# Two-layer hybrid block on one core: the modulation product spread over four column strips from its own ring of buffers, and the last layer's output projection in a written order

## Chip, cores, metric

One core of one Trainium2 chip. The metric is the device time of one execution in microseconds (us).

## The reference

Two layers over 256 latent and 256 context tokens of width 1024. What matters here:

```python
for i in range(DEPTH):
    mod = (s_lat @ ada_w[i] + ada_b[i])          # 1024 -> 6144, one row each for
    mod_c = s_ctx @ ada_w[i] + ada_b[i]          # latent and context
    sh1, sc1, g1, sh2, sc2, g2 = jnp.split(mod, 6, -1)
    u = modulate(h, sh1, sc1)
    # u @ w_in, four token mixers, gates: mix = merged @ w_out
    h = layer_norm(DN_ALPHA * h + g1 * mix, ln1_g[i], ln1_b[i])
    f = conv_ffn(modulate(h, sh2, sc2), ffn_w_up[i], ...)   # up 1024 -> 2*2816, conv, SwiGLU, down
    h = layer_norm(DN_ALPHA * h + g2 * f, ln2_g[i], ln2_b[i])
```

`modulate` is `layer_norm(x) * (1 + scale) + shift`. The last layer computes only the latent tokens from the mixers on (token tiles 2 and 3, 128 tokens each).

## The kernel before

All products with weights are "dense": a weight tile of 128x1024 (512 KB) is loaded by SyncE into the tag `w` (three buffers, `wload`, L190), cut into a rounded high part by ScalarE (`whi`, L197) and a low part by VectorE or GpSimd (`wlo`, L201; two buffers each), and multiplied in three passes per 128 rows of depth: high weight by high activation, high by low, low by high (`mm`, L174). One column tile is 24 matmuls of 512 tokens in layer 0 and of 256 tokens in layer 1.

The modulation (`ada`) is 12 groups per layer. A group is four weight tiles (`adaw`) of 128x1024. Its stationary operand is `sst`, 128x32: only two of its 32 columns are not zero (latent and context). A matmul of it fills one of four strips of 32 columns of the array, and so 32 of 128 partitions of a bank of PSUM. In the kernel before a tile holds two depths k by 512 columns, so that tile c uses strips 0 and 1 or strips 2 and 3:

```python
for k in (2 * c, 2 * c + 1):
    g = k % 4
    self.mm(ps[32 * g:32 * g + 32, :], self.sst[:, k, :], w[:, k % 2 * 512:k % 2 * 512 + 512], k < 4, k >= 4)
yield 0.4
```

After four tiles come a copy (`adas`), four transposes (L178), a sum over the strips (L388) and the bias. `ada` is a generator. `col_tile` draws `rate` steps from it (`self.side`) per column tile of dense work, so that its loads and matmuls stand between those of the dense work, and its tiles use the same three buffers `w`. In layer 0, groups 0 to 3 come first of all, groups 4 to 9 beside the columns of the Hyena and RWKV mixers, and 10 and 11 beside the context's up projection. Layer 1's groups 0 to 3 stand in layer 0's up projection; 4 to 9 beside layer 1's columns for RWKV, Hyena and the window attention; 10 and 11 behind layer 1's output projection, where `backbone` runs them with nothing beside them.

The last layer's output projection (`out_proj`) runs over eight depths for token tiles 2 and 3 and over two halves of 512 columns. `tail` then does for each tile: gate and residual (L1666, L1668), a LayerNorm from sums (`sum_stats`: a square on ScalarE L440, the power -0.5 on GpSimd L443; `post_norm`: L1620, L1625), a second LayerNorm without weights (L455), eight transposes (L178), and scale and shift into `uh` and `ul` (L475, L476, L478). The up projection starts when `uh` and `ul` are there for both tiles. Its first four weight tiles are loaded and cut ahead (`ph`, `pl`).

A scheduler sets the order of the instructions on each engine when the program is built, by its own estimates. Inside `manual_schedule` the engines that are named keep the order in which the program is written. Each engine then runs its own list in order; SyncE's list holds the DMA issues, and a DMA that waits for a buffer holds back those behind it.

Of the kernel before, what the change touches and what calls it, by code (L numbers as in the profile page):

```python
# [8 lines left out]
F32 = mybir.dt.float32  # L9
F32R = mybir.dt.float32r  # L10
# [145 lines left out]
class Net:  # L156
    def __init__(self, ctx, tc, a, out):
        self.ctx, self.tc, self.nc, self.a, self.out = ctx, tc, tc.nc, a, out
        self.work, self.pre, self.pool_cols = [], [], 0
        self.side, self.rate = iter(()), 0  # L160
        self.lo = self.nc.vector
        self.aside, self.done, self.feed = [], set(), None
# [199 lines left out]
    def ada(self, l, groups, early=False):  # L362
# [6 lines left out]
        for g4 in groups:  # L369
            ps = self.bank("d")  # L370
            for c in range(4):
                n = g4 * 4 + c
                tag = ("w", "whi", "wlo", "w", "whi", "w", "wlo")[n % 7] if early else "w"
                w = self.wp.tile([128, 1024], F32, tag=tag, name=tag, bufs=3 if tag == "w" else 2)
                nc.sync.dma_start(w, self.a["adaw"][l, n])
                for k in (2 * c, 2 * c + 1):
                    g = k % 4
                    self.mm(ps[32 * g:32 * g + 32, :], self.sst[:, k, :], w[:, k % 2 * 512:k % 2 * 512 + 512],
                            k < 4, k >= 4)
                yield 0.4  # L380
            sb = self.wp.tile([128, 512], F32, tag="adas", name="adas", bufs=1)
            nc.scalar.copy(sb, ps)
# [16 lines left out]
    def gate_out(self, l, n0, scale):  # L399
# [6 lines left out]
        r = self.wp.tile([16, 128], F32, tag="gr", name="gr", bufs=1)  # L406
# [1296 lines left out]

    def ffn_up(self, l, pool, units, room, hid, hidp, more):
# [36 lines left out]
def backbone(ctx, tc, a, out):  # L1741
# [6 lines left out]
    for l in range(DEPTH):  # L1748
# [5 lines left out]
        N.side = N.ada(l, range(4 if l else 4, 10))  # L1754
        ox = ExitStack()
        if 1:
            with ExitStack() as mx:
# [3 lines left out]
                with ExitStack() as hp:  # L1761
                    qh, qr = [], {}
                    if l:
                        rp = lower()
                        N.rwkv_tiles(l, rp, rp, qr)
                        N.rate = 1
# [4 lines left out]
                        hcx.close()  # L1771
                    hk = hp.enter_context(tc.tile_pool(name="hk", bufs=1, side="right"))
# [74 lines left out]
                    N.rate = (1 if l else 2)  # L1847
# [12 lines left out]
                    N.weave(N.rwkv_prep(l, rp, hq, need_ctx, qr), 0.5)  # L1860
                    N.flush()
# [6 lines left out]
                with ExitStack() as ax:  # L1868
# [6 lines left out]
                    N.weave(N.side, 0.0)  # L1875
                    N.gate_out(l, 16, 0.5)
                    N.rate = 0
# [49 lines left out]
        lg, lb = (op.tile([128, 1024], F32, name=x) for x in ("lg", "lb"))  # L1927
# [16 lines left out]
        def tail(its):  # L1944
            xs = []
            for i, sums in its:
# [8 lines left out]
        N.weave(N.out_proj(l, op, lambda k: a["wout"][l, k], 8, lambda k: ahl[k], tiles, N.h, g1, tail,  # L1955
                           (2 if need_ctx else 5), hooks(), l == 1 and 0), 0.4)
# [145 lines left out]
```

## Time and profile before

| | us |
|---|---|
| median of 3 runs | 1859.11 (1858.53 to 1861.16) |
| the profiled execution | 1862.13 |
| its span, first to last instruction | 1860.1 |
| TensorE matmul (PE) busy | 1702.9 (92%) |
| TensorE weight load (PEld) busy | 1354.4 (73%) |
| VectorE (DVE) busy | 1145.5 (62%) |
| ScalarE (ACT) busy | 787.3 (42%) |
| GpSimd (POOL) busy | 641.4 (34%) |
| HBM read | 235.84 MB, 128 GB/s over the span |

The profiled execution took 2.0 us more than its span, and 3.0 us more than the median. A share of busy time is an average over stages with different limits; a stage is read with the table of stretches and the list of instructions in order of time.

### The profile page before, as it was taken

The numbers are of one execution on the slowest core, as the hardware profiler recorded it, in microseconds if no ns is written. First come the engines' busy times: TensorE is split into PE (matmuls) and PEld (weight loads), VectorE is DVE, ScalarE is ACT, GpSimd is POOL, SyncE is SP. The second block draws the span as 40 slices with busy tenths as digits, with TensorE's granted clock in tenths as the row PEclk, the third lists the DMA queues.
The fourth block names the chain that finished last, engine by engine and source line by source line (L and its number), as shares of the span: only waits on it lengthen the run. The fifth ranks groups of instructions, "written<-read, shape, count | busy, mean of one in ns | idle before, by whom it ended". The sixth has DMA issues, their size and how long they took to land.

```text
span 1860.1 us, 36364 instructions
## 1 busy us (share of the span) xinstructions
PE 1702.9 (92%) x14618; PEld 1354.4 (73%) x14618; DVE 1145.5 (62%) x2204; ACT 787.3 (42%) x1579; POOL 641.4 (34%) x782
## 2 busy tenths in 40 slices
PE   6999999998999988999999998899788998879987
PEld 2566778776777766877787776677687887679964
DVE  5566456775665478544555657563765665758887
ACT  2323345653232346433334444334553343356632
POOL 2313144544544126101010164244454664131153
PEclk9999999999999999999999999999889999889999
DMA  8353321211111455344334556653123222646543
GB/s 302 126 198 113 130 69 57 83 57 45 45 56 55 148 196 189 120 150 139 125 102 138 180 175 210 198 179 130 47 88 97 88 65 82 237 142 189 184 145 113
DMA packets 73456, 241.37 MB, mean 130 GB/s; under 512 B 8518, under 2 KB 17096, under 8 KB 73032
## 3 DMA queue, kind: packets, MB, share of 16 engines
q1 hardware_dynamic: 69336, 229.80, 37.6%
q10 hardware_dynamic: 3952, 9.25, 1.5%
q8 instruction: 115, 1.88, 0.4%
q14 instruction: 53, 0.43, 0.1%
HBM read 235.84 MB, written 2.13 MB: 128 GB/s over the span
## 4 chain that ended last, share of the span: by engine, by line
PE 60%; DVE 15%; ACT 5%; DMA 4%; POOL 3%; issue 3%; POOLq 0%; SPq 0%; ACTq 0%; DVEq 0%
PE bkd L174 45%; PE bkm L174 8%; PE bkm L1362 2%; PE bko L174 2%; DVE wlo L201 2%; PE bkm L178 2%; ACT whi L197 2%; DMA w<-in_wdn 1%; DMA w<-in_wout 1%; DMA w<-in_win 1%; DVE sV L1340 1%; DVE dmx L978 1%; ACT dp L981 1%; POOL wlo L201 1%; DMA w<-in_adaw 1%
## 5 line engine op out<-in xcount | busy, mean ns | idle before, releaser
L174 PE MATMUL bkd<-uh,whi 128*128 128x256 f32 (+1 forms) x1624 | 585.7, 361 | 7.1 <-ACT whi L197 3.3
L174 PE MATMUL bkd<-uh,wlo 128*128 128x256 f32 (+1 forms) x1624 | 555.4, 342 | 3.5 <-DVE wlo L201 3.2
L174 PE MATMUL bkd<-ul,whi 128*128 128x256 f32 (+1 forms) x1624 | 552.9, 340 | 0.0
L197 ACT CAST whi<-w 128x256 fp32r<-128x256 f32 (+1 forms) x532 | 333.7, 661 | 268.4 <-PE bkd L174 116.6
L201 DVE TENSOR_TENSOR wlo<-w,whi 128x1024 fp32r<-128x1024 f32 (+3 forms) x247 | 284.2, 1155 | 195.7 <-ACT whi L197 194.8
L201 POOL TENSOR_TENSOR wlo<-w,whi 128x256 fp32r<-128x256 f32 (+2 forms) x328 | 276.9, 863 | 314.2 <-ACT whi L197 307.6
L174 PEld LDWEIGHTS bkd<-uh,whi 128*128 128x128 f32 x1624 | 311.8, 192 | 85.1 <-ACT whi L197 24.0
L174 PEld LDWEIGHTS bkd<-uh,wlo 128*128 128x128 f32 x1624 | 311.7, 192 | 40.8 <-DVE wlo L201 3.8
L174 PEld LDWEIGHTS bkd<-ul,whi 128*128 128x128 f32 x1624 | 312.9, 193 | 26.6 <-issue 0.7
L1722 POOL TENSOR_TENSOR fc<-fc,fc 128x256 f32<-128x256 f32 (+1 forms) x47 | 46.2, 982 | 331.3 <-DVE fc L329 312.0
L174 PE MATMUL bkd<-w,sst 128*32 128x512 f32 x348 | 81.0, 646 | 18.3 <-DMA w<-in_adaw 18.2
L1584 POOL TENSOR_TENSOR acc<-acc,tg 128x512 f32<-128x512 f32 (+1 forms) x32 | 32.5, 1017 | 145.4 <-DVE tg L1583 132.4
L324 ACT ACTIVATE fc<-bkd,vec 128x256 f32<-128x256 f32 (+1 forms) x94 | 60.8, 647 | 7.5 <-PE bkd L174 7.5
L327 DVE SCALAR_TENSOR_TENSOR fc<-bkd,vec,fc 128x255 f32<-128x255 f32 (+1 forms) x94 | 54.8, 583 | 11.5 <-ACT fc L324 11.5
L174 PE MATMUL bkd<-wlo,hh 128*128 128x512 f32 x126 | 52.4, 416 | 9.3 <-DVE wlo L201 6.2
L237 ACT CAST hh<-fc 128x256 fp32r<-128x256 f32 (+1 forms) x47 | 23.2, 493 | 84.9 <-POOL fc L1722 84.9
L329 DVE SCALAR_TENSOR_TENSOR fc<-bkd,vec,fc 128x255 f32<-128x255 f32 (+1 forms) x94 | 55.3, 589 | 2.9
L238 DVE TENSOR_TENSOR hl<-fc,hh 128x256 fp32r<-128x256 f32 (+1 forms) x47 | 25.6, 545 | 47.4 <-ACT hh L237 47.4
L174 PE MATMUL bkd<-y,wbh 128*128 128x512 f32 (+1 forms) x192 | 54.6, 369 | 0.0
L238 DVE TENSOR_TENSOR wbl<-wb,wbh 128x256 fp32r<-128x256 f32 x48 | 29.3, 611 | 37.0 <-ACT wbh L237 36.7
L174 PE MATMUL bkd<-whi,hh 128*128 128x512 f32 x126 | 48.5, 399 | 3.7 <-DVE fc L329 2.3
L981 ACT ACTIVATE dp<-bkm,dmx 128x512 f32<-128x512 f32 (+1 forms) x48 | 29.6, 617 | 48.2 <-DVE dmx L979 40.2
(474 smaller groups left out, 2995.6 us busy)
## 6 DMA issues: line engine op xcount, KB each, us to landing
w<-in_adaw SPq DMA_DIRECT2D x87, 512.0 KB, 3.9
w<-in_wup SPq DMA_DIRECT2D x82, 512.0 KB, 3.5
w<-in_wdn SPq DMA_DIRECT2D x66, 512.0 KB, 3.5
w<-in_wg SPq DMA_DIRECT2D x64, 512.0 KB, 3.5
w<-in_win SPq DMA_DIRECT2D x58, 512.0 KB, 3.6
w<-in_wout SPq DMA_DIRECT2D x24, 512.0 KB, 3.6
wb<-in_wbr SPq DMA_DIRECT2D x48, 128.0 KB, 3.4
pw<-in_wup SPq DMA_DIRECT2D x8, 512.0 KB, 4.5
```

Of the source, the lines that this page charges most:

```text
L174: self.nc.tensor.matmul(out, lhsT, rhs, start=start, stop=stop)
L178: self.nc.tensor.transpose(out, in_, self.ident[0:n, 0:n])
L197: self.nc.scalar.copy(hi[:, c], w[:, c])
L201: e.tensor_tensor(lo[:, c], w[:, c], hi[:, c].bitcast(F32), ALU.subtract)
L238: nc.vector.tensor_tensor(lo, src, hi.bitcast(F32), ALU.subtract)
L324: nc.scalar.activation(dst, ps, AF.Identity, bias=b, scale=w1)
L327: nc.vector.scalar_tensor_tensor(d3[:, :, 1:256], p3[:, :, 0:255], w0, d3[:, :, 1:256], ALU.mult, ALU.add)
L329: nc.vector.scalar_tensor_tensor(d3[:, :, 0:255], p3[:, :, 1:256], w2, d3[:, :, 0:255], ALU.mult, ALU.add)
L981: nc.scalar.activation(p[:, 0:n], ps[:, 0:n], AF.Exp, scale=scale, bias=mx[:, hc], accum_out=zz[:, hc])
L1362: nc.tensor.matmul(ps[r, o:o + 32], L(r, d, c, x, e, j), R[r, d, 2 * e + j, :], start=True, stop=True, tile_position=(r.start, r.start))
L1584: nc.gpsimd.tensor_tensor(acc, acc, tg[:, 0:n], ALU.add)
L1722: nc.gpsimd.tensor_tensor(ab[0], ab[0], ab[1], ALU.mult)
```

## The change

- `adaw` is packed anew: a tile holds four depths by 256 columns. Each tile gives four matmuls of 256 columns, one for each strip, in place of two of 512 columns on two strips. The bytes, the tiles and the products are the same.
- `ada` can take its tiles from a ring of four buffers of its own (`ew`), and yields after one, two or four tiles (`at_once`). `rate` may be a fraction.
- Layer 0's groups 4 to 9 and layer 1's last groups come from the ring, four tiles at once. Layer 1's groups 0 to 7, not 0 to 3, stand in layer 0's up projection, two tiles at once; groups 8 to 11 stand beside layer 1's Hyena and RWKV columns. Beside layer 1's first six column tiles, and behind its output projection, there are none any more.
- The last layer's `out_proj` and `tail` are replaced by `last_proj`, written out for PE, DVE, ACT and POOL: token tile 2 over all eight depths, then tile 3 by halves; tile 2's norms stand beside tile 3's matmuls; then the first three up tiles on tile 2's 128 tokens, tile 3's norms, and the other 128 tokens of these up tiles (`begun`, drawn by `col_tile`).

The diff, cut to its core:

```diff
     def col_tile(self, src, part):
+        if self.begun:
+            rest_, ps = self.begun.pop(0)
+            yield from rest_
+            return ps
         hi, lo = self.wsplit(src)
-        for _ in range(self.rate):
+        self.due += self.rate
+        while self.due >= 1:
+            self.due -= 1
             next(self.side, None)
...
-                tag = ("w", "whi", "wlo", "w", "whi", "w", "wlo")[n % 7] if early else "w"
-                w = self.wp.tile([128, 1024], F32, tag=tag, name=tag, bufs=3 if tag == "w" else 2)
+                half, h = divmod(c, 2)
+                if ring:
+                    w = ring.tile([128, 1024], F32, tag="ew", name="ew", bufs=4)
...
-                for k in (2 * c, 2 * c + 1):
-                    g = k % 4
-                    self.mm(ps[32 * g:32 * g + 32, :], self.sst[:, k, :], w[:, k % 2 * 512:k % 2 * 512 + 512],
-                            k < 4, k >= 4)
-                yield 0.4
+                for g in range(4):
+                    self.mm(ps[32 * g:32 * g + 32, half * 256:half * 256 + 256], self.sst[:, 4 * h + g, :],
+                            w[:, g * 256:g * 256 + 256], h == 0, h == 1)
...
+                if (c + 1) % at_once == 0:
+                    yield 0.4 * at_once
...
-        N.side = N.ada(l, range(4 if l else 4, 10))
...
+                    ring = hp.enter_context(tc.tile_pool(name="ring", bufs=1, side="right"))
+                    N.side = N.ada(l, range(8, 12) if l else range(4, 10), ring=ring, at_once=4)
...
-                    N.rate = (1 if l else 2)
+                    N.rate = 0.65 if l else 0.8
...
-            N.rate = 1 if l == 0 and kc < k else 2 if part is CTX and k < kc - 1 else 0
+            N.rate = 0.7 if l == 0 and kc < k else 2 if part is CTX and k < kc - 1 else 0
...
-            N.weave(N.ada(l, (10, 11)), 0.0)
-            N.gate_out(l, 40, 1.0)
...
-                    N.side = N.ada(1, range(4))
+                    N.side = N.ada(1, range(8), at_once=2)
...
+            N.last_proj(l, op, fw, ahl, N.h, g1[1], 3)
```

The order of `last_proj` (its helpers do the arithmetic of `out_proj` and `tail`; `cut` loads and cuts one weight tile, `up_cut` a tile of the up projection in quarters, `norms` is a generator over both LayerNorms of a tile):

```python
            self.pool_cols = 256
            cut(0)
            cut(1)
...
            for k in range(8):
                if k < 6:
                    cut(k + 2)
                step(2, k)
            self.pool_cols = 0
            left = [(hf, k) for hf in range(2) for k in range(8)]
            for hf, k in left[:14]:
                step(3, k, [hf])
            cuts = [up_cut(x, nc.vector if x == 1 else nc.gpsimd) for x in range(nup)]
            go(cuts[0])
            gated(2, 0)
            gated(2, 1)
            xn = [P("xn", 1024) for _ in range(2)]
            n2, n3 = norms(2, xn[0]), norms(3, xn[1])
            go(n2, 2)
            go(cuts[1], 1)
            go(n2, 1)
            go(cuts[1])
            go(cuts[2], 2)
            go(n2)
            go(cuts[2])
            gated(3, 0)
            m2 = self.modulate(pool, l, 1, xn[:1], 2)
            next(m2)
            for hf, k in left[14:]:
                step(3, k, [hf])
            go(m2, 6)
            gated(3, 1)
            go(n3, 2)
            go(m2)
            for hi, lo in ups:
                bk = self.bank("d")
                part = lambda c, t0, t1, bk=bk, hi=hi, lo=lo: self.dense(bk[:, c:c + 128], hi, lo, lambda k: k * 128,
                                                                         self.uh, self.ul, 8, t0, t1)
                for _ in part(0, 256, 384):
                    pass
                self.begun.append((part(128, 384, 512), bk[:, 0:256]))
            go(n3)
            for _ in self.modulate(pool, l, 1, xn[1:], 3):
                pass
```

What the change moves, at three places. First SyncE's list in layer 1's columns. The names are target, source: `w<-in_win` is a dense weight tile, `adaw` a modulation tile. Before:

```order
L375 DMA w<-in_adaw 128x1024
L190 DMA w<-in_win 128x1024
L375 DMA w<-in_adaw 128x1024
L190 DMA w<-in_win 128x1024 x2
L375 DMA w<-in_adaw 128x1024
```

and now:

```order
L190 DMA w<-in_win 128x1024 x3
L206 DMA wb<-in_wbr 128x256 x2
L190 DMA w<-in_win 128x1024 x6
L387 DMA ew<-in_adaw 128x1024 x8
L190 DMA w<-in_win 128x1024 x3
L387 DMA ew<-in_adaw 128x1024 x4
L190 DMA w<-in_win 128x1024 x3
L387 DMA ew<-in_adaw 128x1024 x4
L190 DMA w<-in_win 128x1024 x13
```

Where one modulation tile stood before nearly every dense tile, there are now ten dense tiles without one, then eight modulation tiles in a row, and four ahead of every third dense tile.

Second, TensorE's list around the end of the last layer's output projection (`bko` is the half 512 to 1023 of tile 3, `xn` a normed token tile, `ph`/`pl` a cut up tile). Before:

```order
L174 MATMUL bko<-wlo,ah_16895 128x512
L174 MATMUL bko<-whi,al_16896 128x512
L174 MATMUL bkd<-w,sst 32x512 x8
L178 MATMUL bkd<-cstt,adas 128x128 x4
L174 MATMUL bkd<-w,sst 32x512 x4
L178 MATMUL bkm<-cstt,xn 128x128 x8
L174 MATMUL bkd<-w,sst 32x512 x4
L178 MATMUL bkd<-cstt,adas 128x128 x4
L178 MATMUL bkm<-cstt,gt 16x128
L178 MATMUL bkm<-cstt,xn 128x128 x8
L174 MATMUL bkd<-uh_17004,ph_17089 128x256
```

and now:

```order
L174 MATMUL bko<-wh_17344,al_17152 128x512
L178 MATMUL bkm<-cstt,xn 128x128 x8
L174 MATMUL bko<-whi,ah_17153 128x512
L174 MATMUL bko<-wlo,ah_17153 128x512
L174 MATMUL bko<-whi,al_17154 128x512
L174 MATMUL bko<-whi,ah_17155 128x512
L174 MATMUL bko<-wlo,ah_17155 128x512
L174 MATMUL bko<-whi,al_17156 128x512
L174 MATMUL bkd<-uh_17262,ph_17437 128x128
L174 MATMUL bkd<-ul_17270,ph_17437 128x128
```

Tile 2's transposes stand ahead of the last six matmuls of tile 3, the modulation is gone from here, and up tiles start on 128 tokens.

Third, ScalarE's list now, where tile 2 is scaled into `uh` and tile 3 is normed (`h_6989` is tile 3, `lnj` the square):

```order
L488 ACTIVATE uh_17266<-bkm,mod,sc1p 128x128
L488 ACTIVATE uh_17267<-bkm,mod,sc1p 128x128
L197 CAST whi<-w 128x1024 x2
L1772 ACTIVATE lnj,lnve<-h_6989,lnnm 128x1024
L488 ACTIVATE uh_17268<-bkm,mod,sc1p 128x128
L488 ACTIVATE uh_17269<-bkm,mod,sc1p 128x128
L1772 ACTIVATE lnj,lnve<-h_6989,lnnm 128x1024
L1793 ACTIVATE xn<-h_6989,lnns,lnrs 128x512
L488 ACTIVATE uh_17262<-bkm,mod,sc1p 128x128
```

Two casts of later weight tiles and tile 3's first square stand ahead of the last two of tile 2's eight `uh`.

## Rows read from the trace of the kernel before

**Rows 1.** The page, part 1: busy time, share of the span, instructions of an engine.

```profile
PE   1702.9 (92%) x14618; PEld 1354.4 (73%) x14618; DVE 1145.5 (62%) x2204; ACT 787.3 (42%) x1579; POOL 641.4 (34%) x782
```

**Rows 2.** Instructions in order of time, PE, layer 0's up projection (start, us, instruction).

```profile
864.11 0.40 PE L174 MATMUL bkd<-uh,wlo 128*128 128x512 f32 x1
864.44 1.05 PE L174 MATMUL bkd<-w,sst 128*32 128x512 f32 x4
865.42 0.50 PE L174 MATMUL bkd<-uh,whi 128*128 128x512 f32 x1
865.76 0.39 PE L174 MATMUL bkd<-ul,whi 128*128 128x512 f32 x1
```

**Rows 3.** The same view, at the start of the program: three modulation tiles back to back.

```profile
41.37 0.62 PE L174 MATMUL bkd<-w,sst 128*32 128x512 f32 x2
41.38 0.62 PE L174 MATMUL bkd<-wlo,sst 128*32 128x512 f32 x2
...
42.25 1.03 PE L174 MATMUL bkd<-w,sst 128*32 128x512 f32 x4
```

**Rows 4.** Stretches, the modulation's matmuls alone: bounds, length, PE busy, weight loads, DVE, clock, DMA.

```profile
46.00:222.00 176.00, 16.94 (x96) 2.41 (x96) 0.00 (x0) 0.97 0.43 148
780.00:915.00 135.00, 16.83 (x64) 2.30 (x64) 0.00 (x0) 1.00 0.43 143
1125.00:1281.00 156.00, 24.87 (x96) 3.46 (x96) 0.00 (x0) 0.96 0.58 190
```

**Rows 5.** Stretches, all engines: PE, PEld, DVE, ACT, POOL busy, clock, DMA share, GB/s.

```profile
46.00:222.00 176.00, 168.08 (x780) 118.41 (x779) 105.41 (x183) 58.00 (x86) 39.87 (x39) 0.97 0.43 148
1125.00:1281.00 156.00, 139.22 (x891) 107.71 (x890) 96.64 (x196) 65.43 (x116) 60.93 (x65) 0.96 0.58 190
1680.00:1700.00 20.00, 20.00 (x172) 20.00 (x172) 16.57 (x26) 13.41 (x22) 2.23 (x3) 1.00 0.61 188
```

**Rows 6.** Chain of waits over 1125 to 1281 us: shares, and its longest DMA wait.

```profile
by line: PE bkd L174 40.0%; DMA w<-in_win 13.4%; DMA w<-in_adaw 6.3%; issue 4.9%; PE bkm L174 4.6%; ACT whi L197 4.3%; DVE wlo L201 3.8%; POOL wlo L201 2.7%; PE bko L174 2.4%; PE bkm L178 2.3%; DVE hz L615 1.1%; DVE tmp L1150 1.1%; POOL u L
...
1158.98 8.11 DMA w<-in_win
```

**Rows 7.** Instructions in order of time, PE, last output projection to the up projection.

```profile
1590.26 0.40 PE L174 MATMUL bkd<-whi,ah 128*128 128x512 f32 x1
...
1618.75 0.40 PE L174 MATMUL bko<-whi,al 128*128 128x512 f32 x1
...
1642.98 1.97 PE L178 MATMUL bkm<-cstt,xn 128*128 128x128 f32 x8 [2.89 <-POOL xn L455]
1644.86 1.01 PE L174 MATMUL bkd<-uh,ph 128*128 128x256 f32 x3
```

**Rows 8.** The same view there, ACT and DVE; in square brackets the idle time before.

```profile
1595.11 0.41 ACT L1613 CAST ah<-acc 128x256 fp32r<-128x256 f32 x1 [1.64 <-POOL acc L1611]
...
1616.61 1.30 DVE L1666 TENSOR_TENSOR bkd<-bkd,g 128x512 f32<-128x512 f32 x2 [1.68 <-PE bkd L174]
1617.81 0.68 DVE L1668 SCALAR_TENSOR_TENSOR h<-h,bkd 128x512 f32<-128x512 f32 x1
...
1626.88 1.15 ACT L440 ACTIVATE xn<-h,lnnm 128x1024 f32<-128x1024 f32 x1 [1.55 <-DVE lnnm L439]
...
1629.35 1.27 DVE L1620 SCALAR_TENSOR_TENSOR h<-h,lnm,lg 128x1024 f32<-128x1024 f32 x1
...
1632.67 1.50 ACT L475 ACTIVATE uh<-bkm,mod,sc1p 128x128 fp32r<-128x128 f32 x4 [3.42 <-PE bkm L178]
...
1640.64 1.22 DVE L201 TENSOR_TENSOR wlo<-w,whi 128x1024 fp32r<-128x1024 f32 x1
...
1653.04 0.57 ACT L324 ACTIVATE fc<-bkd,vec 128x256 f32<-128x256 f32 x1 [2.19 <-PE bkd L174]
```

**Rows 9.** Instructions in order of time, PE: a single-pass matmul of 128 columns.

```profile
259.73 0.22 PE L174 MATMUL bkm<-msk,idr 128*128 128x128 f32 x1
259.78 0.45 PE L174 MATMUL bkd<-uh,whi 128*128 128x512 f32 x1
```

More of the change, by code (lines that the diff above doesn't have):

```diff
@@ L159, in __init__ @@
         self.work, self.pre, self.pool_cols = [], [], 0
-        self.side, self.rate = iter(()), 0
+        self.side, self.rate, self.due = iter(()), 0, 0.0
         self.lo = self.nc.vector
-        self.aside, self.done, self.feed = [], set(), None
+        self.aside, self.done, self.feed, self.begun = [], set(), None, []
         self.ps = ctx.enter_context(tc.tile_pool(name="ps", bufs=1, space=PSUM))
@@ L360, in rows, with ada @@
         nc.scalar.dma_start(self.row[l], a["row"][l].partition_broadcast(128))
-    def ada(self, l, groups, early=False):
+    def ada(self, l, groups, early=False, ring=None, at_once=1):
         nc, cp = self.nc, self.cp
@@ L1860, in backbone @@
                     N.weave(N.rwkv_prep(l, rp, hq, need_ctx, qr), 0.5)
+                    N.weave(N.side, 0.0)
+                    N.rate = 0
                     N.flush()
@@ L1926, in backbone @@
         op = ox.enter_context(tc.tile_pool(name="op", bufs=1, side="right"))
-        lg, lb = (op.tile([128, 1024], F32, name=x) for x in ("lg", "lb"))
+        if need_ctx:
+            lg, lb = (op.tile([128, 1024], F32, name=x) for x in ("lg", "lb"))
         N.u_tiles()
@@ L1954, in backbone @@
         N.pool_cols = 0 if need_ctx else 0
-        N.weave(N.out_proj(l, op, lambda k: a["wout"][l, k], 8, lambda k: ahl[k], tiles, N.h, g1, tail,
-                           (2 if need_ctx else 5), hooks(), l == 1 and 0), 0.4)
+        if need_ctx:
+            N.weave(N.out_proj(l, op, lambda k: a["wout"][l, k], 8, lambda k: ahl[k], tiles, N.h, g1, tail, 2, hooks(),
+                               False), 0.4)
+        else:
+            N.last_proj(l, op, fw, ahl, N.h, g1[1], 3)
         hid = []
         def more2(k, part):
-            N.rate = 1 if l == 0 and kc < k else 2 if part is CTX and k < kc - 1 else 0
+            N.rate = 0.7 if l == 0 and kc < k else 2 if part is CTX and k < kc - 1 else 0
             if k == NKD // 2:
@@ L2039, in coltiles @@
         return w.reshape(L, 8, 128, n, 128).transpose(0, 3, 2, 1, 4).reshape(L, n, 128, 1024)
-    o["adaw"] = g["ada_w"].reshape(L, 4, 2, 128, 12, 512).transpose(0, 4, 1, 3, 2, 5).reshape(L, 48, 128, 1024)
+    o["adaw"] = g["ada_w"].reshape(L, 2, 4, 128, 12, 2, 256).transpose(0, 4, 5, 1, 3, 2, 6).reshape(L, 48, 128, 1024)
     w = g["w_in"]
```

90 lines of the change are left out of this document (84 added, 6 removed).

## The prediction, made before the changed kernel was run

> **What bounds the kernel now.** I read the page first: the matmul engine is busy for 1702.9 us of the span, 92% [rows 1]. So a saving counts where it takes time from TensorE, or from a stretch in which TensorE waits. Next, the modulation's matmuls in order of time. In layer 0's up projection one modulation tile stands between dense matmuls that otherwise start every 0.229 us. From the dense start at 864.11 to that at 865.76 it takes 1.65 us in place of two steps of 0.229, so a lone tile costs 1.19 us [rows 2]. The third view is the start of the program, where three tiles stand together: the first two, on strips 0, 1 and 2, 3, start within 0.01 us of each other, and the third starts at 42.25, 0.88 us after the first [rows 3]. Four strips therefore take the time that two take. A lone tile leaves two strips empty, and of its 1.19 us some 0.31 is going into the 32-column form and out again.
>
> The stretches tell where that is paid. In 46 to 222 us and 1125 to 1281 us the modulation's matmuls fill 16.94 and 24.87 us, in 780 to 915 us 16.83 [rows 4]. In the first TensorE is busy for 168.08 of 176 us, in layer 1's for only 139.22 of 156, with its DMA engines at 0.58 [rows 5]. The chain of waits says why: 13.4% and 6.3% of those 156 us, 30.7 us, are waits for a dense or a modulation tile, one of them 8.11 us [rows 6]. Both kinds share three buffers there. Last, the end of layer 1's output projection: its last matmul starts at 1618.75, the first of the up projection at 1644.86 [rows 7], 26 us of norms with only eight modulation tiles beside them.
>
> **The change, part by part.** *Four strips.* A tile now fills four strips with 256 columns. Half of 0.88 is 0.44 us a tile (an estimate from [rows 3]), and a run of n tiles costs 0.44 n + 0.31.
>
> *Layer 0's columns.* The 24 tiles stood in 15 runs on TensorE, at most two tiles in each: 15 x 1.19 = 17.9 us, and the stretch's 16.94 agrees, since it leaves out the way in and out [rows 2, 4]. Now six runs of four: 6 x 2.07 = 12.4. Gain **5.5 us**, as TensorE is nearly full there [rows 5]; bounds 2 and 7.
>
> *The start and the context's up projection.* Tiles arrive by DMA; each group ends half a tile earlier. Gain **1 us**, bounds 0 and 2.
>
> *Layer 0's up projection.* 16 lone tiles (19.0 us) become 16 pairs at 2 x 0.44 + 0.31 = 1.19 us (19.0 us) for twice the tiles. Four more groups bring four transposes each, about 1 us by half of the eight at 1642.98 [rows 7], and a way in and out: less than 0.5 us each. Loss **1.8 us**, bounds 1 and 6, since two of three buffers `w` now go to the modulation at a time; what covers this is 5.5 us of dense work for each column tile.
>
> *Layer 1's columns.* 24 tiles in 22 runs were 22 x 1.19 = 26.2 us (24.87 in the stretch, [rows 4]). Now 16 tiles in four runs, 8.3 us, and two groups of transposes fewer, about 1 us: 18.9 us less on TensorE. The DMA waits also shrink: no modulation tile takes a buffer of the dense tiles, and 4 MB fewer are loaded. Against that stand VectorE, busy for 96.64 of the 156 us, and a new wait: eight modulation loads stand in a row on SyncE's list, the second four of them behind the first group's matmuls. I take **19 us**, TensorE's saving and nothing for the DMA waits; bounds 8 (less than half of it) and 30 (the chain's 30.7).
>
> *The tail.* I follow the written order with durations from [rows 7, 8]. ScalarE casts all eight `ah` first, to 1595.5; then one weight tile's high part (1.05) and low part (about 1): first matmul at 1597.5, where before it was 1590.26. Tile 2's 48 matmuls need 11.2 us and wait for weights that come through three buffers: I put their end at 1612.5. Tile 3's first 42 run to 1622.2. Beside them go tile 2's gate and residual (2.7), square (1.15 and its readout 0.2), the two products at 1.27, powers, a second square, and the low parts of two up tiles, which stand in the same lists: `xn` at 1624. TensorE waits 2 us, transposes (1.6), and ends tile 3 at 1627. Tile 3's gate and residual 1.3, two low parts of 1.22 that stand in between on VectorE, its square, the rest of tile 2's `ul`, the second norm: `xn` at 1638. The three up tiles on tile 2 alone are 72 matmuls, which wait for the last two `uh` until 1634 and end at 1640; eight transposes and 0.38 us for each `uh` [rows 8] make tile 3 ready at 1644, with the first up tile's second half beside it. The other two take 48 x 0.116 = 5.6 us [rows 5]: three up tiles are done at 1650. Before, the second was read at 1653.04, and the third 24 x 0.116 = 2.8 us later, at 1655.8. Gain **5.8 us**. Doing the up tiles by halves gains nothing by itself, it only fills the wait: a matmul of 128 columns lets the next one start after 0.05 us [rows 9], but its weight load still sets a step near 0.116, at which both engines are full with 256 columns [rows 5]. Bounds: -3 (the 7 us of later start stay whole and the norms overlap less) and 14 (tile 3's chain runs without the casts in it). The eight modulation tiles that vanish here lay inside the norms and give nothing by themselves.
>
> *Moved with them.* The second gate's transpose and store go to layer 1's window attention, where a single matmul is nothing; the four up tiles cut ahead become three, cut by GpSimd and VectorE beside tile 3.
>
> Sum: 5.5 + 1 - 1.8 + 19 + 5.8 = **29.5 us less** than the profiled 1862.13: 1832.6. That execution is 3.0 us above the median, so I predict **1830 us** for a median against 1859.11.
>
> One cost of the split has no row of its own: twice as many matmuls of half the width. The row that bears on it is the 128-column matmul, after which the next starts in 0.05 us, its bare streaming [rows 9]. The Trainium skill, TensorEngine Tiling (Array Packing), section Instruction Overhead, charges about 60 cycles for each matmul and warns against taking a tiling factor from a dimension that is already small; by it, four more instructions a tile would cost about 0.1 us (an estimate from that page), some 8 us on 80 tiles, and the sum would be 21.5, not 29.5. The trace speaks against it here.
>
> **The rivals.** (1) *The stage and not TensorE.* Layer 1's columns are held by the norms of layer 0's end, by VectorE and by the ring's first loads, and give only 8 us. For it: TensorE idles 16.8 of 156 us there [rows 5]. Against it: DMA waits are the largest foreign share of the chain [rows 6]. 1862.1 - 18.5 - 3 = 1841.
> (2) *Short matmuls pay.* If each of 80 tiles costs 0.1 us more, the bound of a visible fixed cost, 1838. Against it: [rows 9].
> (3) *The tail and the waits both give.* 14 in the tail and 26 in layer 1's columns, 45.7 in all: 1814.
> (4) *The ring blocks the dense tiles*, on the other side. Ten groups of four loads, 2 MB each, now stand as blocks on SyncE's list. Dense tiles behind a block come late, and TensorE stops at each. Price: between nothing and the 8.11 us that a dense tile cost at worst [rows 6]; at 5 us a block, 50 us: 1862.1 - 29.5 + 50 - 3 = 1880. It decides from 2.95 us a block on, which eats the gain. For it: lists are in order. Against it: the ring has its own buffers, so a dense tile no longer waits for a modulation matmul, and two cut tiles are ahead of TensorE; in 46 to 222 us the DMA engines are only 0.43 busy [rows 5].
> (5) *The strips do not do it.* Should four strips with four streams from one tile not overlap as two tiles did, a tile would keep 0.88 us and only fewer runs be left: layer 0's columns lose 5 us, its up projection another 14, layer 1's columns gain 10, the tail 6: 1856. Against it: [rows 3].
>
> **How the numbers follow.** Forecast 0.60, with its own range of 1820 to 1840; rival 1 0.15, rival 2 0.05, rival 3 0.10, rival 4 0.07, rival 5 0.03. A measurement of this kernel tells about 0.2%, 3.7 us, from no change. All but rival 4 are faster by more, save half of rival 5: faster 0.90. Rival 4 lies between no change and slower: slower 0.07, within 0.2% 0.03. For 8 in 10 the range takes in rivals 1 to 3 and the bounds of the tail and of layer 1: **1812 to 1848**.
>
> **What would show it.** Modulation matmuls of 256 columns with some 0.44 us a tile and about 1.8 us between the first and the last start of a run of four; some 12 us of them in layer 0's columns in place of 17, 8 in layer 1's in place of 25, and none behind the output projection. In layer 1's columns hardly any wait for `adaw` or `in_win`, and a stretch near 137 us. From the start of the output projection to the third up tile's end 60 us in place of 65.5, with up matmuls of 128 columns before tile 3's transposes. The prediction is wrong if dense matmuls wait for weights behind blocks of `ew` loads, if the strips run one after the other, or if layer 1's columns stay near 150 us.

## The result and the profile after

The changed kernel is slower. In runs taken in turn on one chip its median is 1879.7 us (1875.1 to 1884.1, 4 runs), the kernel before has 1860.1 (1858.5 to 1865.2, 4 runs): a ratio of 1.0102, 95% interval 1.0076 to 1.0128. The forecast was 1830, with a range of 1812 to 1848. The profiled execution took 1880.6 us.

The page after: busy time of each engine, and the granted TensorE clock in 40 slices of 47 us.

```profile
PE 1701.4 (91%) x15074; PEld 1393.1 (74%) x15074; DVE 1138.6 (61%) x2207; ACT 789.4 (42%) x1590; POOL 652.3 (35%) x796
...
PEclk9899999989999999999999998999889999769999
```

TensorE's busy time hardly fell [rows 1]. The strips did what they promised; next the modulation's matmuls alone, in the stretches of [rows 4], layer 1's moved by the 7 us that it begins later:

```profile
46.00:222.00 176.00, 11.60 (x192) 5.81 (x192) 0.00 (x0) 0.96 0.42 149
780.00:915.00 135.00, 10.71 (x160) 4.17 (x160) 0.00 (x0) 1.00 0.48 164
1132.00:1288.00 156.00, 10.13 (x128) 3.65 (x128) 0.00 (x0) 0.90 0.48 165
```

They fill 11.60 us in place of 16.94 in layer 0's columns, 10.13 in place of 24.87 in layer 1's, and 10.71 in place of 16.83 in a piece of layer 0's up projection, there with 20 tiles in place of 16. So some 26 us of TensorE's work vanished from these three stretches and came back as something else. The last digits of the clock's row say where to look: a 7 and a 6 from 1597 to 1691 us, where the kernel before has two 8s.

Where the time went is read from instructions that both kernels have: their starts, and the time between two of them, in one profiled execution of each.

| from the row above to | before | after | time between, before and after | differs by | forecast |
|---|---|---|---|---|---|
| ScalarE's first copy dxq, behind layer 0's columns | 262.01 | 258.36 | 262.0, 258.4 | -3.7 | -6.0 |
| last matmul with ah of layer 0's output projection | 714.50 | 714.28 | 452.5, 455.9 | +3.4 | 0 |
| SyncE's store of layer 0's second gate (context's up projection) | 748.65 | 753.70 | 34.2, 39.4 | +5.3 | -0.5 |
| first matmul of layer 0's down projection | 993.27 | 1000.47 | 244.6, 246.8 | +2.2 | +1.8 |
| its last matmul but one | 1125.42 | 1132.21 | 132.2, 131.7 | -0.4 | 0 |
| ScalarE's first copy dxq of layer 1, behind its columns | 1296.41 | 1303.07 | 171.0, 170.9 | -0.1 | -19 |
| first of TensorE's last transposes of osb, ahead of the branch | 1580.17 | 1584.83 | 283.8, 281.8 | -2.0 | 0 |
| ScalarE's read of the fourth up tile | 1658.89 | 1677.37 | 78.7, 92.5 | +13.8 | -5.8 |
| the end | 1860.1 | 1878.8 | 201.2, 201.4 | +0.2 | 0 |

The first forecast is the 5.5 us of the columns and half of the 1 us for start and context. Pieces of 2 or 3 us in one execution are no finding: E2 and E7 below are the kernel before up to 1630 and 1680 us, and between two such marks their profiled executions ran up to 2 us apart from it, E7's 5 us in layer 1's attention. But the 3.4 us of the second row come again in the other five runs that keep the changed kernel's order there (2.9 to 3.9 us in E1, E3, E6, E8 and E9; 0.7 and 2.6 in E10 and E11), some 2 us of them between 668 and 705 us. What layer 0's columns gained is gone by its output projection, and why stays open. Three more rows ask for a cause: the context's up projection, layer 1's columns and the tail.

**The tail.** TensorE in order of time, at tile 2's share of the first up tile:

```profile
1636.57 0.28 PE L174 MATMUL bkd<-uh,ph 128*128 128x128 f32 x1
1641.82 0.47 PE L174 MATMUL bkd<-ul,ph 128*128 128x128 f32 x1 [4.97 <-DVE ul L491]
1642.09 0.41 PE L174 MATMUL bkd<-uh,pl 128*128 128x128 f32 x1
```

Up to here the order had won: the first up matmul stands at 1634.70 where it stood at 1644.86 [rows 7]. Then come 5 us without work, and behind them a matmul starts every 0.213 us, not every 0.116 as ahead of them. ScalarE and VectorE say what TensorE waited for:

```profile
1634.88 0.81 ACT L488 ACTIVATE uh<-bkm,mod,sc1p 128x128 fp32r<-128x128 f32 x2 [0.21 <-DVE ul L491]
1635.58 1.98 ACT L197 CAST whi<-w 128x1024 fp32r<-128x1024 f32 x2
1640.08 1.15 ACT L1772 ACTIVATE lnj<-h,lnnm 128x1024 f32<-128x1024 f32 x1 [2.52 <-DVE lnm L1773]
...
1641.23 0.78 ACT L488 ACTIVATE uh<-bkm,mod,sc1p 128x128 fp32r<-128x128 f32 x2
```

The last two uh of tile 2 stand behind tile 3's square, and that waits for VectorE, whose list has two 1.22 us low parts, at 1637.50 and 1638.70, ahead of its lnm at 1639.90. The stretches of 4 us show what the wait left behind (columns as in [rows 5]):

```profile
1632.00:1636.00 4.00, 3.64 (x25) 3.18 (x25) 2.85 (x9) 3.53 (x10) 3.33 (x8) 1.00 0.29 83
1636.00:1640.00 4.00, 0.85 (x8) 0.70 (x7) 3.97 (x9) 1.56 (x2) 0.21 (x1) 0.73 0.23 89
1640.00:1644.00 4.00, 1.96 (x8) 1.77 (x9) 3.19 (x7) 1.93 (x4) 1.26 (x3) 0.50 0.75 248
...
1672.00:1676.00 4.00, 4.00 (x23) 4.00 (x23) 0.96 (x2) 0.98 (x2) 0.00 (x0) 0.58 0.00 0
1676.00:1680.00 4.00, 4.00 (x37) 4.00 (x36) 2.10 (x3) 2.27 (x3) 0.22 (x1) 1.00 0.04 16
```

The granted clock falls to 0.50, the 1.2 GHz level, in the wait. It stays there through the 128-column matmuls, the last of which starts at 1671.65, and rises at about 1675, 3.3 us after the first of 256 columns. In the kernel before TensorE also came out of a wait at 0.50, but to matmuls of 256 columns, and their step fell to 0.116 us some 4 us after the first:

```profile
1644.00:1648.00 4.00, 4.00 (x18) 3.55 (x17) 2.68 (x8) 2.91 (x8) 2.84 (x8) 0.50 0.18 73
1648.00:1652.00 4.00, 4.00 (x32) 4.00 (x31) 0.60 (x2) 0.56 (x1) 0.00 (x0) 0.85 0.72 267
```

**Layer 1's columns.** SyncE's list of loads there, and TensorE:

```profile
1136.27 21.59 SPq L190 DMA_DIRECT2D w<-in_win  x6
1161.45 16.10 SPq L387 DMA_DIRECT2D ew<-in_adaw  x8
1177.60 6.79 SPq L190 DMA_DIRECT2D w<-in_win  x3
```

```profile
1160.10 0.28 PE L174 MATMUL bkd<-uh,wlo 128*128 128x256 f32 x1
1167.21 1.08 PE L174 MATMUL bkd<-ew,sst 128*32 128x256 f32 x8 [6.83 <-DMA ew<-in_adaw]
1168.23 0.58 PE L174 MATMUL bkd<-uh,whi 128*128 128x256 f32 x1
```

and what TensorE waited for by DMA in 1132 to 1288 us (in total, times, longest):

```profile
PE bkd L174 <- DMA ew<-in_adaw: 8.7, 2, 6.8
```

Eight ring loads, 4 MB, stand in one row, and no dense tile is sent for between 1157.9 and 1177.6 us. But TensorE does not wait for a dense tile's load. Its list has the ring's first matmuls in the middle of a column tile, and it comes to them behind 1160.10, ahead of the first ring load, which is sent at 1161.45 behind six dense ones. So it waits 6.83 us for the first ring tile and 1.88 for the next, and works at a granted clock of 0.50 from 1168 to 1177 us. Behind the block, from 1177 to 1200 us, it works without a gap. Instructions that start 5.5 us later than in the kernel before at 1155 us (its time) start 18.8 later at 1162, and 10.5 later at 1173, since the kernel before stands still there as well (8.11 us [rows 6]). The price of the place is better read against E6 below, where only the ring's steps differ: matmuls that start 0.3 us earlier than E6's at 1154 us start 14.5 later at 1179, and 15.6 later behind the columns.

**The context.** ScalarE's list at 740 us:

```profile
739.80 2.20 ACT L488 ACTIVATE uh<-bkm,mod,sc1p 128x128 fp32r<-128x128 f32 x6 [1.03 <-PE bkm L178]
742.54 0.81 ACT L488 ACTIVATE uh<-bkm,mod,sc1p 128x128 fp32r<-128x128 f32 x2 [0.54 <-DVE ul L491]
743.25 0.39 ACT L237 CAST hh<-fc 128x256 fp32r<-128x256 f32 x1
743.54 0.59 ACT L393 COPY adas<-bkd 128x512 f32<-128x512 f32 x1
```

```profile
744.18 1.12 PE L178 MATMUL bkd<-cstt,adas 128*128 128x128 f32 x4 [3.53 <-ACT adas L393]
```

In the kernel before, the copy adas was ahead of the eight casts uh:

```profile
739.63 0.59 ACT L382 COPY adas<-bkd 128x512 f32<-128x512 f32 x1 [0.42 <-PE bkd L174]
```

It is behind them now; four transposes of it, and all dense work behind them, wait 3.53 us.

### The profile page after: what moved, and what is told of

Its sections match the earlier page's. It is cut to its first block, busy times and chain, and to the rows that moved or that the text cites. A ratio compares the mean times of both kernels' runs of the same rounds, so it can differ in the third digit from the quotient of the medians.

```text
span 1878.8 us, 37323 instructions
## 1 busy us (share of the span) xinstructions
PE 1701.4 (91%) x15074; PEld 1393.1 (74%) x15074; DVE 1138.6 (61%) x2207; ACT 789.4 (42%) x1590; POOL 652.3 (35%) x796
## 5 line engine op out<-in xcount | busy, mean ns | idle before, releaser
L201 DVE TENSOR_TENSOR wlo<-w,whi 128x1024 fp32r<-128x1024 f32 (+3 forms) x245 | 270.2, 1108 | 193.7 <-ACT whi L197 192.4
L174 PEld LDWEIGHTS bkd<-uh,whi 128*128 128x128 f32 x1632 | 316.1, 194 | 57.0 <-issue 14.7
L174 PEld LDWEIGHTS bkd<-uh,wlo 128*128 128x128 f32 x1632 | 315.8, 194 | 47.4 <-DVE wlo L201 7.7
L174 PEld LDWEIGHTS bkd<-ul,whi 128*128 128x128 f32 x1632 | 316.9, 194 | 26.7 <-issue 1.0
L174 PE MATMUL bkd<-whi,hl 128*128 128x512 f32 x126 | 51.0, 406 | 0.0
```

Source lines behind the costliest of these rows:

```text
L174: self.nc.tensor.matmul(out, lhsT, rhs, start=start, stop=stop)
L201: e.tensor_tensor(lo[:, c], w[:, c], hi[:, c].bitcast(F32), ALU.subtract)
```

## The experiments

Each was profiled, and E1 to E6 and E9 to E11 were timed in turn with the kernel before on their chip; ratios are to that kernel's median there (1861.6 to 1864.9). The changed kernel's own ratio is 1.0102; "by the two ratios" compares a run's ratio with it. E7 and E8 have one execution each.

**E1. The up tiles whole.** In the changed kernel:

```
-            for hi, lo in ups:
...
-                self.begun.append((part(128, 384, 512), bk[:, 0:256]))
+            self.pre.extend(tuple(hl) for hl in ups)
```

> The changed kernel, with the three up tiles done whole (256 columns) after tile 3's transposes, in place of 128 columns at a time; the rest of the written order stays. In the changed kernel TensorE ran at the lower level (1.2 GHz) from 1640 to 1674 us, and that ended with the last 128-column matmul. Theory A, the 128-column matmuls hold TensorE at the lower level: here the dense work begins near 1650 at 1.2 GHz as in the kernel before (there 1644 to 1649), is back at 2.4 GHz some 5 us later, and the third up tile is done near 1661 in place of 1674: 13 us faster than the changed kernel, 1866. Theory B, the 1.2 GHz comes from the wait for the last uh and lasts whatever TensorE does then: the 1.2 GHz goes on to about 1674 with whole matmuls, which by then would have done the three tiles (72 x 0.213 = 15 us) and half of the next three, and the time falls by about 4 us, to 1875.

1869.6 us, a ratio of 1.0030 (1.0007 to 1.0053): 0.7% or 13 us faster than the changed kernel by the two ratios, as theory A has it. The third up tile was read at 1658.31 us, in the changed kernel at 1672.11. From the transposes of osb to the fourth up tile it took 0.1 us less than the kernel before, where the changed kernel took 13.8 more. The stretches:

```profile
1644.00:1648.00 4.00, 2.36 (x10) 2.05 (x11) 0.76 (x2) 1.80 (x4) 0.85 (x3) 0.50 0.01 4
1648.00:1652.00 4.00, 4.00 (x25) 3.78 (x25) 2.80 (x8) 1.95 (x6) 2.47 (x8) 0.69 0.02 7
1652.00:1656.00 4.00, 4.00 (x35) 4.00 (x35) 0.74 (x2) 1.13 (x2) 0.00 (x0) 1.00 0.99 383
```

Although TensorE now idles for longer ahead of tile 3, the clock is back within some 5 us of dense work. E3 and E6 below, which keep the halves, lose 12.8 and 12.9 us in the tail; E9, which does not, 0.3.

**E2. The same halves in the kernel before.** Tiles 0, 1 and 2 of layer 1's up projection:

```
+            yield from self.dense(ps[:, 0:128], hi, lo, lambda k: k * 128, self.uh, self.ul, 8, 256, 384)
+            yield from self.dense(ps[:, 128:256], hi, lo, lambda k: k * 128, self.uh, self.ul, 8, 384, 512)
```

> The kernel before, with the first three up tiles of layer 1 alone done as two runs of 24 matmuls of 128 columns in place of one of 24 of 256; both runs stand after tile 3's transposes, so nothing waits that did not wait before. Theory A (128-column matmuls hold TensorE at 1.2 GHz): 144 matmuls x 0.213 us = 31 us from 1645 on, in place of the 11 us that the three tiles take in the kernel before (24 at 0.213, 48 at 0.116): 20 us slower, 1880, with a granted clock of 0.50 up to about 1675. Theory B (they do not, and only double the number of weight loads): the clock rises after some 5 us as before, 24 x 0.213 + 120 x 0.116 = 19 us in place of 11: 8 us slower, 1868.

1876.1 us, 1.0071 (1.0045 to 1.0097): 13 us slower, between the two, and by the trace theory A. At the end of the output projection this execution was 3.3 us ahead of the kernel before, at the fourth up tile 14.4 behind: 17.7 us lost (20 expected), of which some 2 came back later. Not all of the 144 matmuls stood behind tile 3's transposes, as was expected: 20 went ahead of them, 15 of these at full clock. The other 124 ran from 1642.7 to 1669.3 us, with TensorE busy without a gap:

```profile
1644.00:1648.00 4.00, 4.00 (x21) 4.00 (x20) 2.22 (x7) 1.35 (x4) 1.83 (x6) 0.50 0.21 33
...
1668.00:1672.00 4.00, 4.00 (x23) 4.00 (x24) 0.96 (x2) 0.98 (x2) 0.00 (x0) 0.60 0.00 0
1672.00:1676.00 4.00, 4.00 (x37) 4.00 (x36) 0.97 (x2) 0.78 (x2) 0.73 (x1) 1.00 0.00 0
```

**E7. The halves at full clock.** The edit of E2 on tiles 16, 17 and 18.

> The kernel before, with the up tiles 16, 17 and 18 of layer 1 done as two runs of 128 columns each, in the middle of the dense stretch, where TensorE has long been at 2.4 GHz. Theory A1, 128-column matmuls keep whatever level they find: the clock stays at 1.00 and the three tiles take 144 x 0.116 = 16.7 us in place of 8.4: 8 us slower. Theory A2, they bring the clock down too: it falls to 0.50 inside these 144 matmuls, and each then takes 0.213: up to 31 us, 15 to 22 us slower.

One execution, 1865.0 us. The clock did not fall:

```profile
1688.00:1692.00 4.00, 4.00 (x38) 4.00 (x38) 1.22 (x4) 1.77 (x3) 0.73 (x1) 1.00 0.43 147
```

From 7.0 us ahead of the kernel before to 0.6 behind across these tiles: 7.6 us, theory A1's 8 for twice the weight loads. So here the same matmuls kept the level that they found.

**E8. The last uh first.** In the written order of the changed kernel:

```
-            go(m2, 6)
+            go(m2)
             gated(3, 1)
             go(n3, 2)
-            go(m2)
```

> The changed kernel, with tile 2's last two uh ahead of tile 3's second gate, residual and square in the written order. In the changed kernel TensorE waited 5 us for them (1637 to 1641.8 us) and came out of the wait at 1.2 GHz. Theory A, the wait starts the lower level and the 128-column matmuls hold it: the 72 matmuls on tile 2 go on without a stop at 0.116 us and end near 1643, TensorE then waits for tile 3's norm till about 1650 and does the second halves at 1.2 GHz, 72 x 0.213 = 15 us: the third up tile is done near 1666 in place of 1674, 8 us faster. Theory B, the first halves bring the clock down by themselves: they take up to 15 us, no wait is left before tile 3, and the third up tile is done no earlier than 1670.

One execution, 1874.3 us; the third up tile was read at 1665.73, theory A's 1666. TensorE's stretches show first halves at full clock, then the wait for tile 3, then second halves at 0.50:

```profile
1636.00:1640.00 4.00, 4.00 (x38) 4.00 (x37) 4.00 (x9) 2.15 (x3) 0.79 (x3) 1.00 0.24 95
1640.00:1644.00 4.00, 3.03 (x28) 2.88 (x26) 3.26 (x7) 1.25 (x2) 0.55 (x1) 0.99 0.82 236
1644.00:1648.00 4.00, 0.10 (x1) 0.10 (x2) 1.52 (x7) 2.06 (x3) 0.56 (x1) 0.50 0.05 18
...
1664.00:1668.00 4.00, 4.00 (x20) 4.00 (x21) 1.25 (x3) 0.98 (x2) 0.00 (x0) 0.52 0.00 0
```

With E1, E2 and E7 this shows what happened in the tail: the level fell in a wait, and the 128-column matmuls behind it ran at the lower level to their end.

**E3. Layer 1's columns without modulation.**

```
-                    N.side = N.ada(l, range(8, 12) if l else range(4, 10), ring=ring, at_once=4)
+                    N.side = iter(()) if l else N.ada(l, range(4, 10), ring=ring, at_once=4)
...
-                    N.side = N.ada(1, range(8), at_once=2)
+                    N.side = N.ada(1, range(12), at_once=2)
```

> The changed kernel, with all twelve groups of layer 1's modulation in layer 0's up projection (one step of two tiles for each column tile) and none in layer 1's columns: no ring there. The columns stage (1132 to 1288 us in the changed kernel, 156 us) then holds no modulation tile at all. Theory A, the ring's loads block the dense tiles: PE's wait of 6.8 us for ew and the stall of 13 us at 1160 to 1180 go, with the 10 us of modulation matmuls: the stage falls to about 133 us. Theory B, the stage is held by VectorE, GpSimd and the dense weights' own loads: the stall goes but the stage stays above 145 us. Layer 0's up projection takes about 4 groups x 3 us more. By A some 10 us faster than the changed kernel (1870), by B 2 us slower to 3 us faster.

1885.7 us, 1.0116 (1.0075 to 1.0158). From the down projection's last matmul to layer 1's first dxq it took 155.5 us in place of 170.9, 15.3 less, which by the expectation's measure is a stage of 141: between the theories. For that, instructions that stood 1.5 us later than in the changed kernel at 755 us, ahead of layer 0's up projection, stood 14.7 later at 1008, behind it: 3.3 us for each of the four groups. So the tiles cost nearly as much where TensorE is full as with their wait in the columns, and the time as a whole, within the noise of the changed kernel's (some 3 us above it by the two ratios), comes nearest to theory B's. Without any modulation the columns still took some 141 us in this execution.

**E6. The ring later.** In the changed kernel, for layer 1:

```
-                    N.rate = 0.65 if l else 0.8
+                    N.rate, N.due = (0.8, -3.0) if l else (0.8, 0.0)
```

> The changed kernel, with layer 1's first ring group four column tiles later (the steps begin at a debt of 3, then go at 0.8 a tile in place of 0.65). On SyncE's list stand then two ew loads, a dense tile, two ew, three dense, where eight ew loads stood in a row before the next dense tile. Theory A, this block at 1161 to 1177 us is what the columns lost: the wait of 6.8 us for ew and the half-speed matmuls behind it go, and the stage falls from 156 to about 149 us (141 without any modulation tile, and 16 tiles at 8.3): the time 7 us below the changed kernel, 1873. Theory B, the stage's second half is held by VectorE and GpSimd and takes any such gain back: the stall goes, but the window attention begins within 2 us of where it did.

1867.3 us, 1.0026 (1.0011 to 1.0041), by the two ratios 0.75% or 14 us under the changed kernel: theory A, with twice its size. The same marks are 155.0 us apart, 15.9 less, with all 16 tiles inside. SyncE's list and the stretch that answers to the changed kernel's 1132 to 1288:

```profile
1136.55 21.62 SPq L190 DMA_DIRECT2D w<-in_win  x6
1161.77 0.82 SPq L387 DMA_DIRECT2D ew<-in_adaw  x2
1164.42 0.33 SPq L190 DMA_DIRECT2D w<-in_win  x1
1164.80 0.93 SPq L387 DMA_DIRECT2D ew<-in_adaw  x2
1170.37 7.39 SPq L190 DMA_DIRECT2D w<-in_win  x3
```

```profile
1132.00:1272.00 140.00, 120.51 (x916) 105.97 (x915) 94.02 (x192) 64.08 (x115) 60.15 (x63) 0.98 0.54 180
```

TensorE's first ring matmuls now stand at 1170.28 and 1177.71 and wait for nothing. What the order of the loads gave and what the later place of the matmuls on TensorE gave was not separated by a run. The traces speak for the place: the first ring load goes out at the same time in both (1161.45 and 1161.77), TensorE comes to its matmul 10 us later, and no matmul in the changed kernel's columns waited for the load of a dense tile. Of the 16 us, the profiled execution gave back 6.7 in layer 1's attention and down projection, in pieces of 1 to 3 us.

**E4. The strips alone.** The kernel before, with the new packing and

```
-                for k in (2 * c, 2 * c + 1):
...
+                half, h = divmod(c, 2)
+                for g in range(4):
```

> The kernel before, with the new packing of adaw and its matmuls alone: four strips of 256 columns a tile, one tile at a time at the places where tiles stood before, no ring, the old output projection. Theory A, the strips pay wherever TensorE is busy: a lone tile costs 0.44 + 0.31 in place of 1.19 us, so 24 tiles in layer 0's columns give 10 us, 16 in its up projection 7, and of layer 1's columns between 0 and 10: 17 to 27 us faster than the kernel before, 1833 to 1843. Theory B, of a lone tile the way in and out of the 32-column form is most of the cost: 5 us faster or less, 1855 or more.

1858.3 us, 0.9975 (0.9957 to 0.9992): 4.7 us, theory B's size, for another reason than B's. Where TensorE is full the forecast's price holds: layer 0's up projection came out 6.6 us shorter with its 16 lone tiles, 0.41 each. In order of time:

```profile
864.88 0.40 PE L174 MATMUL bkd<-uh,wlo 128*128 128x512 f32 x1
865.20 0.64 PE L174 MATMUL bkd<-w,sst 128*32 128x256 f32 x8
865.77 0.50 PE L174 MATMUL bkd<-uh,whi 128*128 128x512 f32 x1
866.10 0.39 PE L174 MATMUL bkd<-ul,whi 128*128 128x512 f32 x1
```

1.22 us from dense start to dense start in place of 1.65 [rows 2]. Layer 1's columns gave 4.8. Layer 0's gave 1.9 with the start, where theory A had 10; why so little stays open. And the context lost 5.5 us here too, with no ring and no new order anywhere near, by the same wait:

```profile
743.83 1.11 PE L178 MATMUL bkd<-cstt,adas 128*128 128x128 f32 x4 [3.53 <-ACT adas L382]
```

**E5. The strips, the context's groups earlier.**

```
-            N.side, N.rate = N.ada(0, (10, 11)), 2
+            N.side, N.rate = N.ada(0, (10, 11)), 3
```

> The kernel with the strips alone, and one number more: beside the context's up projection of layer 0 the modulation goes three tiles for each column tile in place of two, so that its second group ends before the tokens' modulate, not in the middle of it. With the strips alone, as in the changed kernel, TensorE stood there for 3.5 us: four transposes waited for ScalarE's copy adas, which stood behind eight casts uh in its list, and the next matmuls ran at 1.2 GHz; 5.5 us against the kernel before. Theory A, that order is the whole loss: 5.5 us come back, 10 us faster than the kernel before (a ratio of 0.9945). Theory B, the copy then stands in the way of an earlier norm: between 0 and 3 us come back, a ratio of 0.996 or more.

1859.2 us, 0.9985 (0.9970 to 0.9999), theory B. At the down projection it is 3.2 us ahead of E4, but 2.0 of that stands already at the output projection, ahead of the edit, and nothing of it is left at the end. The copy's wait is down to 0.7 us; in its place TensorE waits 5.40 us for a modulation tile. Beside the context 4.3 us are lost in place of 5.5.

**E9. Three repairs at once** in the changed kernel: E1, E6 and E5's number.

> The changed kernel with three repairs together: the up tiles whole after tile 3 (as with the whole tiles alone), layer 1's ring four column tiles later, and the modulation beside layer 0's context three tiles for each column tile. Theory A, the three losses are separate and add up: 12 us for the tail, 12 for the ring as it stood at the end of the layer, 3 for the copy: 1880 - 27 = 1853, a ratio to the kernel before near 0.996, and the columns, the tail's clock and the copy's wait each as in the run that repaired it alone. Theory B, something else in the changed kernel costs the same time again once a wait goes (the later start of the output projection, the two more groups in layer 0's up projection): 1862 or more, a ratio of 1.001 or more.

1856.4 us, 0.9966 (0.9953 to 0.9980), theory A in the sum: 1.4% under the changed kernel, 25 us by the ratios and 27 expected. Its parts are not all as in the single runs. The columns took 160.7 us between E6's marks, 6 more than in E6 alone; beside the context 4.0 us were lost, 1.3 less than in the changed kernel, with a wait of 4.90 us for a modulation tile as in E5; and the third up tile was read 9.9 us ahead of the kernel before.

**E10. Put together from both.** The changed kernel with the old output projection, norms and last two groups, the ring late, single tiles in layer 0's up projection, and E5's number:

```
-            N.last_proj(l, op, fw, ahl, N.h, g1[1], 3)
+            N.weave(N.out_proj(l, op, lambda k: a["wout"][l, k], 8, lambda k: ahl[k], tiles, N.h, g1, tail,
...
+                    N.side = N.ada(l, range(4, 10), ring=ring, at_once=4)
+                    N.rate, N.due = (1, -4.0) if l else (0.8, 0.0)
+                    N.side = N.ada(1, range(4))
```

> Put together from both kernels: the four strips everywhere; the ring in both layers' columns, in layer 1 five column tiles late and with its six groups (4 to 9) as in the kernel before; single tiles in layer 0's up projection (four groups of layer 1); the last two groups in the last output projection's norms, and that projection and its norms as in the kernel before; three tiles for each column tile beside layer 0's context. Theory A: 3.7 us from layer 0's columns, 6.6 from its up projection (16 single tiles at 0.41 less), 10 to 16 from layer 1's columns, 3 lost in between: 17 to 23 us faster than the kernel before, a ratio of 0.988 to 0.991. Theory B, six groups don't fit where four did: the columns of layer 1 last 150 us again, 8 us faster or less, a ratio of 0.9955 or more.

1847.7 us, 0.9920 (0.9891 to 0.9950): 15 us faster than the kernel before, the lowest median of all, between the theories and nearer to A. The profiled execution shows 6.4 us by the first dxq, 6.6 in layer 0's up projection, 10.4 in layer 1's columns, with 4 lost beside the context. Six groups did fit.

**E11. One tile for each of the context's.** E10 with 1 in place of 3.

> The kernel put together from both, with one number changed: one modulation tile for each of the context's six column tiles in place of three; the other two tiles of its last group follow when these are done. The loss of 4 us at 720 to 740 us that the kernel put together still has against the kernel before is, by its trace, a wait of 5.3 us for modulation tiles: three loads in a row before each dense tile. Theory A, that is the whole of it, and the copy adas comes when no cast uh is ahead of it: the stretch gives 4 us back, a ratio to the kernel before near 0.990. Theory B, the two tiles that are left over, with their transposes and the gate's store behind the context, cost what the wait did: within 1 us, a ratio of 0.9915 to 0.993.

1851.9 us, 0.9952 (0.9933 to 0.9971): above both theories, and the 4 us that were hoped for are not there. Its median is above E10's, but the two intervals overlap. Beside the context 5.3 us were lost, with three tiles 4.0 and with two (E4) 5.5. What it would take was not found.

## Why the prediction was wrong, step by step

- *Four strips, 0.44 us a tile, 0.31 for a run.* Right: a run of four is one row of 1.93 us, and E4's lone tile costs 0.41 us less, where 0.44 was said.

```profile
1184.57 1.93 PE L174 MATMUL bkd<-ew,sst 128*32 128x256 f32 x32
```

- *Layer 0's columns, 5.5 us and part of the 1.* 3.7 measured, in the bounds; E4 and E10 gave 1.9 and 6.4. The forecast carried the gain to the end; in the changed kernel 0.2 of it is left at layer 0's output projection. *Up projection, a loss of 1.8:* 2.2 measured.
- *Start and context, a gain of 1.* The context lost 5.3 us. The step costed an order that the forecast had not looked at: which of ScalarE's operations stands first when a group ends in the middle of a modulate. E4 shows that the packing alone brings it about.
- *Layer 1's columns, 19 us.* Zero. The size was nearly right: 15.9 us with the ring late (E6), 15.3 with no tile at all (E3). The step that failed is the overlap of the ring's loads with TensorE's work: the new wait was named (eight loads in a row, four of them behind the first group's matmuls) and set at nothing. TensorE came to the first ring tile before its load was sent, waited 8.7 us in all for ring tiles and worked on at half clock; about 15 us went there (against E6). The first group also did not come as one run of four tiles but as four lone ones. Rival 4 has a fitting total, 1880, by luck: it puts 5 us on each of ten blocks, for dense tiles that come late behind them. No matmul waited for the load of a dense tile, one place cost about 15 us, and the table shows no loss of that kind at the others.
- *The tail, 5.8 us.* It lost 13.8. The order of events was forecast within some 5 us: counted from the transposes of osb, which stand 4.7 us later than before, the first out projection matmul came at 1596.0 (1597.5 forecast), the last at 1629.8 (1627), the first up matmul at 1630.0, tile 3's xn at 1643.2 (1638). What failed above all is "the other two take 48 x 0.116" and the 72 before them: the forecast had a wait for the last two uh and put no clock behind it. Of 144 matmuls 16 ran at full clock; 128 x (0.213 - 0.116) = 12.4 of the 19.6 us between forecast and measurement. The rest was not taken apart; the late xn lies in it. E1, which has no halves to slow down but no longer fills the wait either, gains 0.1 us in this stretch and not 5.8. The row with the half clock in the kernel before was there to be read, at 1644 to 1649.
- *Rival 2, short matmuls pay.* Not as said: in the strips a fixed cost of each instruction does not show. In the halves each matmul of 128 columns took 0.11 us at full clock (E7), as long as one of 256, which the forecast had in its step of 0.116. What it lacked was the level of the clock. The rule of the Trainium skill that was weighed, TensorEngine Tiling (Array Packing), section Instruction Overhead, would by the forecast's estimate have put 0.1 us on a tile; E4's rows leave room for 0.03.
- On the rise of the clock, the profile's rows come first: 1.2 GHz for some 26 us of unbroken 128-column matmuls in E2, and 2.4 GHz 2 us after 256-column ones follow. The Trainium skill, TensorE: Matmul & The Clock Gate, section The HAM clock gate, says that the number of matmuls does not matter for the rise, which comes with sustained work. E2's unbroken work, some 120 matmuls (26 / 0.213), saw no rise; the measurement decides.
- The experiments nearly add up: tail 13 and ring 14 by their ratios, context 1 by its marks, and E9, with all three, is 25 us faster than the changed kernel.
- Two sums of the rivals are off; the forecast does not rest on them, only half of rival 5's chance of 0.03 does. Rival 3's terms make 44.7 us, which its 1814 goes with, not 45.7. Rival 5's gains and losses make a loss of 3 us, 1862, not 1856.

What stays open: why the scheduler puts the copy adas behind the uh with the new packing, and a place for the context's groups that costs nothing; where layer 0 loses its columns' gain; what part of E6's gain, if any, is SyncE's order.

## What to carry to other kernels

A saving on the bounding engine is worth what the waits around it let through: before a block of loads is put into an in-order list, look at when its first load goes out and when its first use comes up. Work that fills a wait should keep the matrix engine's clock in view: here 128-column matmuls behind a wait ran at the lower level to their end, 26 us in E2, where 256-column ones were out of it within 5. A written order needs the last operation of one tile ahead of the first of the next on every engine, not only on the one that is being filled.

## What the runs showed of the hardware

Matmuls of 128 columns, each with its own weights, ran at a granted clock of 0.50 for as long as they lasted (1642.7 to 1669.3 us in E2; 1641.8 to 1671.9 in the changed kernel, with eight transposes among them), at 0.213 us each; the clock rose 2.0 and 3.3 us after the first matmul of 256 columns. The same matmuls begun at a granted clock of 1.00 kept it (E7), 38 of them in 4 us. Matmuls of 256 columns after the same kind of wait saw 1.00 again within some 5 us (the kernel before, E1).
